# Row maxima of two query heads from one pair of 64-row products, in a two-layer hybrid mixer on one core

## The chip, the cores and the metric

The kernel runs on one core of one Trainium2 chip. The metric is device time in microseconds (us), the median of several runs; less is better.

## What is computed

The reference is two layers over 2048 latent tokens behind a prefix of 256 context tokens, model width 1024. Each layer normalises and modulates the tokens, projects them once, feeds four token mixers (Fourier, attention, short convolution, pooling), gates each with a SiLU path and sends all through one output projection. What the change touches is the attention: 4 query heads of width 64 on 2 key/value heads, latent queries reading all 2304 keys in one softmax.

```python
sc = jnp.einsum('bqkgd,bskd->bkgqs', qi, k_all, preferred_element_type=jnp.float32)
p = jax.nn.softmax(sc, axis=-1).astype(v_all.dtype)
return jnp.einsum('bkgqs,bskd->bqkgd', p, v_all)
```

## The kernel before, in words

Every fp32 operand is split into a high and a low fp16 part, and a product is made of several fp16 products. The tokens are five blocks: block 0 is the 256 context tokens, blocks 1 to 4 hold 512 latent tokens each. In layer 0 attention runs for blocks 1, 2, 3, 4, 0, in layer 1 for blocks 1 to 4.

Attention of one head on one block has two parts. `Head.front` (line 910) loads the head's queries (tile `qb`: high, high, low parts, 192 columns a token), transposes the first 128 columns (line 917) into `qhh` with 128 rows (the high part twice), and finds each query's maximum over all keys: for each of the four groups of 128 queries, five products (line 926) of `qhh` with the keys, one of 256 context keys (`kc`) and four of 512 (`kst`). A key tile has 128 rows, the high part over the low part, so one 128-row product sums query-high by key-high and query-high by key-low. Each product goes into a bank of the pool `mx`, which has two buffers of one bank, and VectorE reduces it to one column of `mp` (line 927). Then the five columns are reduced (line 930), scaled into column 192 of `qb` (line 931), and four more transposes (line 934) give `qlm`, 65 rows: the low query part and the maximum, which one further copy (line 936) brings to SBUF. `Head.main` (line 945) then goes over 18 key tiles of 128 keys: two score products (lines 967 and 968, the second reads `qlm`), two exponentials on ScalarE (`ph` line 972, `p32` line 973), a subtraction on GpSimd or VectorE (`pl`, line 974), and products with the values (lines 962 and 960).

`attention` (line 1014) weaves the heads: while head i runs its `main`, the `front` of head i+1 is advanced at key tiles 0, 2, 4, 7, 10 and 13, a group of 128 queries (five products) at a time, so the last piece of the front comes five key tiles ahead of its use. `spread` (line 1172) weaves in a fill: projections of the other mixers (line 307), later the output projection (line 1120). `opening` (line 1193) starts the first front while the last keys and values of the layer are still being brought in by `keys_values`. In the end a scheduler that simulates the engines sets the order of the instructions on each engine from these streams; each engine then runs its own list in order.

The other names in the change: `gain` and `cd` are constant tiles held for the whole kernel, `z` the buffers of the gate projections, `ot` a buffer of the output projection, `PSHIFT` the headroom that is added to the maximum, `kd` the keys in HBM.

Of the kernel before, what the change touches and what calls it, by code (L numbers as in the profile page):

```python
# [10 lines left out]
F32 = mybir.dt.float32  # L11
# [8 lines left out]
DEPTH = 2  # L20
# [15 lines left out]
PSHIFT = 13.0 * math.log(2.0)  # L36
# [6 lines left out]
def hybrid_kernel(ctx: ExitStack, tc: tile.TileContext, T, out):  # L43
# [12 lines left out]
    banks = {tag: pool("ps_" + tag, 2, space=PSUM) for tag in ("st", "mx", "pv", "fl")}  # L56

    def ring(*tags):
        i = [0]

        def bank(dt=F32):
            i[0] += 1
            tag = tags[i[0] % len(tags)]
            return banks[tag].tile([128, 2048 // mybir.dt.size(dt)], dt, tag=tag, name=tag)

        return bank
# [13 lines left out]
    kd = tc.dram_tile([18, 128, 256], F16, name="kd")  # L80
# [24 lines left out]
    gain = const.tile([128, DEPTH, 4, 64], F32, name="gain")  # L105
    edge = const.tile([128, 2, 16], F32, name="edge")
    invw = const.tile([128, 2], F32, name="invw")
    cd = const.tile([128, 2, 128], F32, name="cd")
# [235 lines left out]
    def token_groups(L, tp, ws):  # L344
# [27 lines left out]

        gm = sm.tile([128, 1], F32, tag="gm", name="gm")
        DVE.tensor_reduce(out=gm, in_=gain[:, L, 0, :], axis=AX.X, op=ALU.max, apply_absolute_value=True)
# [6 lines left out]
        gq = tp.tile([128, 4, 64], F32, tag="gq", name="gq")  # L381
        DVE.tensor_scalar(out=gq[:, 0:2], in0=gain[:, L, 0:2], scalar1=gs, scalar2=None, op0=ALU.mult)
        DVE.tensor_scalar(out=gq[:, 2:4], in0=gain[:, L, 2:4], scalar1=gk, scalar2=None, op0=ALU.mult)
# [45 lines left out]
        def keys(w, b, table):  # L429
            g0, n = BLK[b]  # L430
            nt = n // 128
            q3 = normed(tok_major(w[0], b).rearrange("p t (h f) -> p t h f", h=2), w[1], table)
            o = tp.tile([128, 4, 2, 2, 64], F16, tag="ko", name="ko")[:, 0:nt]
            oh = o[:, :, :, 0, :].rearrange("p t h f -> p (t h) f")
            ol = o[:, :, :, 1, :].rearrange("p t h f -> p (t h) f")
            ACT.copy(out=oh, in_=q3)
            POOL.tensor_tensor(out=ol, in0=q3, in1=oh, op=ALU.subtract)
            SP.dma_start(out=kd[g0 // 128:(g0 + n) // 128].rearrange("t p c -> p t c"), in_=o.rearrange("p t h s f -> p t (h s f)"))
# [221 lines left out]
    def fourier(L, tp):  # L660
        def ub(shape, dt, name):
            return tp.tile(shape, dt, tag="u", name=name)

        wf = ub([128, 2, 256], F32, "wf")
# [192 lines left out]
    def keys_values(L, tp, kvs):  # L857
# [19 lines left out]
        for b in range(5):  # L877
# [3 lines left out]
            kr = tp.tile([128, 4, 256], F16, tag="zt", name="kr")[:, 0:nt]  # L881
            SP.dma_start(out=kr, in_=kd[t0:t0 + nt].rearrange("t p c -> p t c"))
            for kv in range(2):
                pt = mx_bank(F16)
                for t in range(nt):
                    mark[0] = PE.transpose(out=pt[:, t * 128:(t + 1) * 128], in_=kr[:, t, kv * 128:(kv + 1) * 128], identity=id16).ins
                if b == 0:
                    ACT.copy(out=kc_[:, 0, kv, :], in_=pt[:, 0:n])
                    DVE.tensor_copy(out=kc_[0:64, 1, kv, :], in_=pt[0:64, 0:n])
                else:  # L890
                    ACT.copy(out=kst[kv][:, g0 - NCTX:g0 - NCTX + n], in_=pt[:, 0:n])
                    DVE.tensor_copy(out=k2[kv][0:64, g0 - NCTX:g0 - NCTX + n], in_=pt[0:64, 0:n])
# [8 lines left out]

    class Head:


        def __init__(self, L, kvs, b, h, tp):
            self.L, self.kvs, self.b, self.h, self.tp = L, kvs, b, h, tp

        def front(self):
            b, h, tp, kvs = self.b, self.h, self.tp, self.kvs
            g0, n = BLK[b]  # L910
            nt = n // 128
            kv = h // 2
            qb = tp.tile([128, 4, QW], F16, tag="qb", name="qb")[:, 0:nt]
            load_mark[0] = SP.dma_start(out=qb[:, :, 0:192], in_=qd[g0 // 128:(g0 + n) // 128, :, h].rearrange("t p c -> p t c")).ins
            pt = mx_bank(F16)
            for t in range(nt):
                PE.transpose(out=pt[:, t * 128:(t + 1) * 128], in_=qb[:, t, 0:128], identity=id16)
            qhh = tp.tile([128, 512], F16, tag="qhh", name="qhh")[:, 0:n]
            ACT.copy(out=qhh, in_=pt[:, 0:n])
            yield  # L920
            keys = [kvs["kc"][:, 0, kv, :]] + ([] if b == 0 else [kvs["kst"][kv][:, i * 512:(i + 1) * 512] for i in range(4)])
            mp = sm.tile([128, 4, 5], F32, tag="mp", name="mp")
            for t in range(nt):
# [5 lines left out]
            mr = sm.tile([128, 4], F32, tag="mr", name="mr")[:, 0:nt]  # L929
            DVE.tensor_reduce(out=mr, in_=mp[:, 0:nt, 0:len(keys)], axis=AX.X, op=ALU.max)  # L930
            DVE.tensor_scalar(out=qb[:, :, 192], in0=mr, scalar1=-1.0 / MROW, scalar2=PSHIFT * LOGIT / MROW, op0=ALU.mult, op1=ALU.add)
            pt = mx_bank(F16)
            for t in range(nt):
                PE.transpose(out=pt[0:65, t * 128:(t + 1) * 128], in_=qb[:, t, 128:193], identity=id16)
            qlm = tp.tile([128, 512], F16, tag="qlm", name="qlm")[:, 0:n]
            DVE.tensor_copy(out=qlm[0:65, :], in_=pt[0:65, 0:n])
            self.q = qhh, qlm
# [7 lines left out]
        def main(self):  # L945
# [4 lines left out]
            qhh, qlm = self.q  # L950
# [35 lines left out]
        def back(self, o32):  # L986
# [3 lines left out]
            if h % 2 == 0:  # L990
                o32[0] = tp.tile([128, 4, 128], F32, tag="o32", name="o32")[:, 0:nt]
            o = o32[0]
# [6 lines left out]
        def close(self, o32):  # L999
# [3 lines left out]
            o = o32[0]  # L1003
            if h % 2:
                j = h // 2
                zt = tp.tile([128, 512], F32, tag="zt", name="zt")[:, 0:n]
# [7 lines left out]
    def attention(heads):  # L1014

        o32 = [None]
        for _ in heads[0].front():
            yield
        for i, hd in enumerate(heads):
            ahead = heads[i + 1].front() if i + 1 < len(heads) else iter(())  # L1020
            for j, _ in enumerate(hd.main()):
                if j == 1 and i:
                    heads[i - 1].back(o32)
                if j == (1 if heads[i].b == 0 else 3) and i:
                    heads[i - 1].close(o32)
                if hd.b == 0 or j in (0, 2, 4, 7, 10, 13):
                    next(ahead, 0)
                yield
            yield from ahead
        heads[-1].back(o32)  # L1030
        heads[-1].close(o32)
# [60 lines left out]
    def project(L, blocks, tp):  # L1092
# [13 lines left out]
        for i, tok in enumerate(toks):  # L1106
# [9 lines left out]
            for half in range(2):  # L1116
# [8 lines left out]
                ot = tp.tile([128, 512], F32, tag="ot", name="ot")  # L1125
# [230 lines left out]
```

## Time and profile before

| | |
|---|---|
| median of 3 runs | 2284.16 us (2273.7 to 2284.55) |
| the profiled execution's own time | 2278.62 us |
| its span, first to last instruction | 2276.8 us |
| TensorE busy | 2169.0 us, 95% of the span |
| VectorE busy | 1401.3 us, 62% |
| ScalarE busy | 1228.4 us, 54% |
| GpSimd busy | 929.4 us, 41% |
| mean granted TensorE clock | 0.979 of full |

In the rows further down PE is TensorE's matmul part, PEld its weight loads, DVE VectorE, ACT ScalarE, POOL GpSimd, SP the queue that issues most DMAs. A matmul's shown duration contains its way through the pipeline, so the distance between two starts is what a matmul takes from the engine, and the duration is when its result is there.

### The profile page before, as it was taken

The numbers are of one execution on the slowest core, as the hardware profiler recorded it, in microseconds if no ns is written. First come the engines' busy times: TensorE is split into PE (matmuls) and PEld (weight loads), VectorE is DVE, ScalarE is ACT, GpSimd is POOL, SyncE is SP. The second block draws the span as 40 slices with busy tenths as digits, with TensorE's granted clock in tenths as the row PEclk, the third lists the DMA queues.
The fourth block names the chain that finished last, engine by engine and source line by source line (L and its number), as shares of the span: only waits on it lengthen the run. The fifth ranks groups of instructions, "written<-read, shape, count | busy, mean of one in ns | idle before, by whom it ended". The sixth has DMA issues, their size and how long they took to land.

```text
span 2276.8 us, 41305 instructions
## 1 busy us (share of the span) xinstructions
PE 2169.0 (95%) x16327; PEld 1296.6 (57%) x16327; DVE 1401.3 (62%) x2639; ACT 1228.4 (54%) x2297; POOL 929.4 (41%) x996
## 2 busy tenths in 40 slices
PE   7998999989998999999999989999999999899999
PEld 3997556545555555545557984554454555455554
DVE  3655686366768767666465546413567767687743
ACT  4653453346777666544545625323467666566640
POOL 2786443214444455422226861011344556333320
PEclk9999999999999999999999999999999999899999
DMA  8423455510322111223473424323124210222133
GB/s 316 149 87 120 148 183 177 176 57 24 108 83 81 45 36 33 91 86 110 147 241 124 136 73 139 112 104 103 35 70 143 68 37 31 65 72 73 61 116 120
DMA packets 164081, 237.97 MB, mean 105 GB/s; under 512 B 28618, under 2 KB 113966, under 8 KB 163886
## 3 DMA queue, kind: packets, MB, share of 16 engines
q1 hardware_dynamic: 141294, 205.95, 27.2%
q10 hardware_dynamic: 22592, 29.37, 4.2%
q8 instruction: 128, 2.10, 0.4%
q14 instruction: 67, 0.55, 0.1%
HBM read 165.94 MB, written 69.34 MB: 103 GB/s over the span
## 4 chain that ended last, share of the span: by engine, by line
PE 75%; DVE 8%; POOL 6%; ACT 5%; DMA 3%; issue 3%; SPq 0%; POOLq 0%; ACTq 0%; DVEq 0%
PE fl L307 19%; PE fl L1120 15%; PE st L307 6%; PE pv L962 4%; PE st L967 4%; PE mx L926 4%; PE st L968 4%; PE pv L329 3%; PE st L329 3%; PE pv L960 2%; DVE mp L927 2%; PE st L319 2%; PE pv L319 2%; PE mx L848 1%; PE fl L169 1%
## 5 line engine op out<-in xcount | busy, mean ns | idle before, releaser
L307 PE MATMUL fl<-h,w 128*128 128x512 f16 (+1 forms) x2592 | 585.4, 372 | 12.5 <-ACT w L147 8.9
L974 POOL TENSOR_TENSOR pl<-p,ph 128x512 f16<-128x512 f32 (+1 forms) x292 | 360.4, 1234 | 566.1 <-ACT p L973 488.5
L307 PEld LDWEIGHTS <-w 128*128 128x128 f16 x3456 | 332.3, 99 | 376.6 <-issue 23.7
L972 ACT ACTIVATE ph<-st 128x512 f16<-128x512 f32 (+1 forms) x584 | 350.9, 601 | 233.4 <-PE st L968 225.0
L927 DVE TENSOR_REDUCE mp<-mx 128x1 f32<-128x512 f32 (+1 forms) x648 | 390.2, 627 | 123.6 <-PE mx L926 115.7
L1120 PE MATMUL fl<-wo,ml 128*128 128x512 f16 x1632 | 376.5, 379 | 1.3 <-DVE ml L148 0.8
L973 ACT ACTIVATE p<-st 128x512 f32<-128x512 f32 (+1 forms) x584 | 351.5, 602 | 30.2 <-DVE pl L974 22.7
L974 DVE TENSOR_TENSOR pl<-p,ph 128x512 f16<-128x512 f32 (+1 forms) x292 | 232.5, 796 | 123.5 <-ACT p L973 103.5
L1120 PEld LDWEIGHTS <-ml 128*128 128x128 f16 x1632 | 157.4, 98 | 181.7 <-DVE ml L148 1.4
L962 PE MATMUL pv<-V,ph 128*128 128x130 f16 x2320 | 231.1, 222 | 6.3 <-ACT ph L972 5.8
L962 PEld LDWEIGHTS <-ph 128*128 128x128 f16 x2320 | 170.9, 98 | 115.5 <-ACT ph L972 27.7
L926 PE MATMUL mx<-kst,qhh 128*128 128x512 f16 x512 | 192.3, 387 | 21.6 <-DVE mp L927 20.7
L967 PE MATMUL st<-qhh,kst 128*128 128x512 f16 x512 | 196.4, 384 | 6.4 <-ACT p L973 5.6
L968 PE MATMUL st<-qlm,k 65*128 65x512 f16 x512 | 197.4, 386 | 0.0
L307 PE MATMUL st<-h,w 128*128 128x512 f16 (+1 forms) x864 | 191.0, 372 | 0.0
L960 PE MATMUL pv<-V,pl 128*128 128x66 f16 x2320 | 173.0, 194 | 11.7 <-POOL pl L974 5.8
L960 PEld LDWEIGHTS <-pl 128*128 128x128 f16 x2320 | 134.8, 98 | 63.7 <-POOL pl L974 12.1
L329 PEld LDWEIGHTS <-h 128*128 128x128 f16 x1632 | 159.4, 98 | 19.5 <-POOL h L269 0.7
L319 PEld LDWEIGHTS <-h 128*128 128x128 f16 x1728 | 98.9, 98 | 1.3 <-issue 0.6
L926 PEld LDWEIGHTS <-qhh 128*128 128x128 f16 x648 | 62.9, 99 | 63.2 <-issue 24.0
L329 PE MATMUL pv<-w,h 128*128 128x256 f16 x816 | 94.3, 274 | 0.4 <-POOL h L269 0.4
L269 POOL TENSOR_TENSOR h<-h,h 128x512 f16<-128x512 f32 x72 | 85.3, 1189 | 18.3 <-ACT h L268 17.4
(303 smaller groups left out, 2906.1 us busy)
## 6 DMA issues: line engine op xcount, KB each, us to landing
wm<-in_w_mod_dram SPq DMA_DIRECT2D x48, 512.0 KB, 4.7
wst<-in_w_in_dram SPq DMA_DIRECT2D x44, 512.0 KB, 4.8
mix<-mixd SPq DMA_DIRECT2D x34, 512.0 KB, 4.2
zd<-z SPq DMA_DIRECT2D x64, 256.0 KB, 2.2
wst<-in_w_out_dram SPq DMA_DIRECT2D x32, 512.0 KB, 4.8
xt<-in_x_dram SPq DMA_DIRECT2D x20, 512.0 KB, 4.8
xd<-xt SPq DMA_DIRECT2D x18, 512.0 KB, 2.9
xt<-xd ACTq DMA_DIRECT2D x18, 512.0 KB, 3.6
```

What stands on the lines that cost most here:

```text
L307: PE.matmul(out=ps, lhsT=w[:, wp, k, :], rhs=h_ap(b, hp, k, 0, n), start=(k == 0 and i == 0), stop=(k == KC - 1 and i == 2))
L329: PE.matmul(out=ps[:, t], lhsT=h_ap(b, hp, k, (2 * i + t) * 128, 128), rhs=w[:, :, wp, k, :], start=(k == 0 and j == 0), stop=(k == KC - 1 ...
L926: mark[0] = PE.matmul(out=ps, lhsT=qhh[:, t * 128:(t + 1) * 128], rhs=kk, start=True, stop=True).ins
L927: DVE.tensor_reduce(out=mp[:, t, i:i + 1], in_=ps, axis=AX.X, op=ALU.max)
L960: PE.matmul(out=pv[t // 2][:, t % 2, 0:66], lhsT=p, rhs=v[:, 0:66], start=False, stop=(kt == nk - 1), skip_group_check=True)
L962: PE.matmul(out=pv[t // 2][:, t % 2, :], lhsT=p, rhs=v, start=(kt == 0 and t % 2 == 0), stop=False, skip_group_check=True)
L967: mark[0] = PE.matmul(out=ps, lhsT=self.k_tile(0, kt), rhs=qhh, start=True, stop=False).ins
L968: PE.matmul(out=ps, lhsT=self.k_tile(1, kt)[0:65, :], rhs=qlm[0:65, :], start=False, stop=True)
L972: ACT.activation(out=ph, in_=ps, func=ACTF.Exp, scale=1.0 / LOGIT)
L973: ACT.activation(out=p32, in_=ps, func=ACTF.Exp, scale=1.0 / LOGIT)
L974: (POOL if kt % 2 == 0 else DVE).tensor_tensor(out=pl, in0=p32, in1=ph, op=ALU.subtract)
L1120: PE.matmul(out=ps, lhsT=ml[:, mp, k, :], rhs=wo[k][:, wp, half * 512:(half + 1) * 512], start=(k == 0 and j == 0), stop=(k == KC - 1 and ...
```

## The change

A class `Pair` takes the place of `Head.front`. It makes the front of two query heads, i and i+2, which belong to the two key/value heads. The key tile of head 1 is turned over (low part over high part, which needs the high part once more in HBM: `kd` has 320 columns for 256), so that key head 0 has its high part in rows 0 to 63 and key head 1 in rows 64 to 127. The maximum is now taken over the products of the high parts alone, 64 rows each: head i in the upper half of the array, head i+2 in the lower, into the two banks of one tile, and one reduction takes the maxima of both. The low part is left out of the maximum, and `PSHIFT` goes from 13 to 10 powers of two. `mx` becomes one buffer of two banks during attention (`mx_mode`). The front advances one pair of products at a time, spread over both heads' key tiles. Three front steps, no longer one, go with each step of `opening`. `qb` has one buffer (of two heads), `z` and `pw` one, `gain` and `cd` are loaded anew in each layer, and `ot` is gone (the product with the gate is written back to PSUM). Line numbers from here on with 948, 949, 957 and the like are those of the changed kernel.

```diff
-PSHIFT = 13.0 * math.log(2.0)
+PSHIFT = 10.0 * math.log(2.0)
...
+    def mx_mode(name, wide):
+        mx_scope.close()
+        p = mx_scope.enter_context(tc.tile_pool(name="ps_mx" + name, bufs=1 if wide else 2, space=PSUM, reuse_waits="tile"))
+        banks["mx"], banks["size"] = p, 4096 if wide else 2048
...
+            DVE.tensor_copy(out=o[:, :, 256:320], in_=pairs[:, :, 1, 0, :])
...
+            def turned(c, m):
+                pt = pv_bank(F16)
                 for t in range(nt):
-                    mark[0] = PE.transpose(out=pt[:, t * 128:(t + 1) * 128], in_=kr[:, t, kv * 128:(kv + 1) * 128], identity=id16).ins
+                    mark[0] = PE.transpose(out=pt[0:m, t * 128:(t + 1) * 128], in_=kr[:, t, c:c + m], identity=id16).ins
+                return pt
+            pt = turned(0, 128)
+            ACT.copy(out=both[0], in_=pt[:, 0:n])
+            DVE.tensor_copy(out=high[0][0:64], in_=pt[0:64, 0:n])
+            pt = turned(192, 128)
+            ACT.copy(out=both[1], in_=pt[:, 0:n])
+            pt = turned(128, 64)
+            DVE.tensor_copy(out=high[1][0:64], in_=pt[0:64, 0:n])
...
+    class Pair:
+        def __init__(self, b, i, tp, kvs):
+            self.b, self.heads, self.tp, self.kvs = b, (i, i + 2), tp, kvs
+            self.nt, self.nk = BLK[b][1] // 128, 1 if b == 0 else 5
+            self.steps = 1 + self.nt * self.nk
...
+            mp = sm.tile([128, 2, 4, 5], F32, tag="mp", name="mp")
+            for t in range(nt):
+                for j in range(nk):
+                    ps = mx_bank().rearrange("p (h c) -> p h c", h=2)[:, :, 0:512 if j else NCTX]
+                    for i in range(2):
+                        kk = kvs["kst"][i][:, (j - 1) * 512:j * 512] if j else kvs["kc"][:, 0, i, :]
+                        r = slice(64 * i, 64 * i + 64)
+                        mark[0] = PE.matmul(out=ps[:, i], lhsT=qhh[r, i, t * 128:(t + 1) * 128], rhs=kk[r], start=True, stop=True).ins
+                    DVE.tensor_reduce(out=mp[:, :, t, j], in_=ps, axis=AX.X, op=ALU.max)
+                    yield
...
-            for t in range(nt):
-                for i, kk in enumerate(keys):
-                    ps = mx_bank()[:, 0:kk.shape[-1]]
-                    mark[0] = PE.matmul(out=ps, lhsT=qhh[:, t * 128:(t + 1) * 128], rhs=kk, start=True, stop=True).ins
-                    DVE.tensor_reduce(out=mp[:, t, i:i + 1], in_=ps, axis=AX.X, op=ALU.max)
-                yield
...
-                if hd.b == 0 or j in (0, 2, 4, 7, 10, 13):
-                    next(ahead, 0)
-                yield
-            yield from ahead
+                    at += 1
+                    while done < want * at // (total - 1):
+                        next(ahead, 0)
+                        done += 1
+                    yield
...
-        for i, _ in enumerate(load):
-            if i < 5:
-                steps(att, 1)
+        for _ in load:
+            steps(att, 3)
             yield 1
...
-        ap = TagPool(right, tc, f"a{L}", {"zt": 2, "p32": 2, "qb": 2, "qhh": 2, "qlm": 2, "ph": 3, "pl": 3, "acc": 1, "o32": 1}, "right")
+        ap = TagPool(right, tc, f"a{L}", {"zt": 2, "p32": 2, "qb": 1, "qhh": 2, "qlm": 2, "ph": 3, "pl": 3, "acc": 1, "o32": 2}, "right")
+        mx_mode(f"a{L}", True)
```

The order moves at two places that matter below. The first is TensorE's list while attention opens in layer 0. Names: `kst` and `kc` are keys, `qhh` queries, `w` a weight of the fill, `h` its tokens; what stands in brackets is the engine that is waited for. Before:

```order
L926 LDWEIGHTS qhh
L926 MATMUL mx<-kst_5482,qhh 128x512 [waits DVE_49]
L926 LDWEIGHTS qhh
L926 MATMUL mx<-kst_5482,qhh 128x512 [waits DVE_49]
L307 LDWEIGHTS w
L307 MATMUL fl<-h_322,w 128x256
```

The change, at the same stage:

```order
L948 LDWEIGHTS qhh
L948 MATMUL mx<-kst_5494,qhh 128x512 [waits DVE_49]
L948 LDWEIGHTS qhh
L948 MATMUL mx<-kst_5495,qhh 128x512
L948 LDWEIGHTS qhh
L948 MATMUL mx<-kst_5494,qhh 128x512 [waits DVE_49]
L948 LDWEIGHTS qhh
L948 MATMUL mx<-kst_5495,qhh 128x512
L315 LDWEIGHTS w
L315 MATMUL fl<-h_318,w 128x256
```

Two products that fill the two buffers became two products that fill one; the next pair waits for VectorE to have read both. In the changed list the 324 pairs stand in 304 runs: 293 single pairs and 11 runs of two to four pairs, with 21 places where a pair stands straight behind another; 20 of these places are in the two openings.

The second place is TensorE's list where a front ends and the next one begins. `qb` is loaded by DMA, `id` is the identity of a transpose. Before, four transposes to `qlm` (line 934), at once the four of the next head's `qb`, then fill:

```order
L934 LDWEIGHTS qb
L934 MATMUL mx<-id_98,qb 65x128
L917 LDWEIGHTS qb [waits DMAHW7_49]
L917 MATMUL mx<-id_98,qb 128x128
L917 LDWEIGHTS qb
L917 MATMUL mx<-id_98,qb 128x128
L917 LDWEIGHTS qb
L917 MATMUL mx<-id_98,qb 128x128
L917 LDWEIGHTS qb
L917 MATMUL mx<-id_98,qb 128x128
L307 LDWEIGHTS w
L307 MATMUL fl<-h_1461,w 128x512 [waits Activation_49]
```

The change, at one of its 20 such places (line 957 is what line 934 was, 998 what 968 was, 992 what 962 was, 937 what 917 was):

```order
L957 LDWEIGHTS qb
L957 MATMUL mx<-id_98,qb 65x128
L998 LDWEIGHTS kc
L998 MATMUL st<-qlm,kc 128x512 [waits DVE_49]
L998 LDWEIGHTS kc
L998 MATMUL st<-qlm,kc 128x512
L992 LDWEIGHTS ph [waits Activation_49]
L992 MATMUL pv<-V_5485,ph 128x130 [waits PE_49]
```

Behind these rows come three more products of line 992 and then the transposes of line 937, whose `qb` can be loaded only when the transposes of line 957 have read the one buffer. The score products that read `qlm` now follow its transposes directly, and the next load and its use stand within a few products of each other.

## Rows read from the trace of the kernel before

**Rows 1.** The page: busy time of TensorE's matmuls, and the chain that ended last.

```profile
PE 2169.0 (95%) x16327; PEld 1296.6 (57%) x16327; DVE 1401.3 (62%) x2639; ACT 1228.4 (54%) x2297; POOL 929.4 (41%) x996
...
PE 75%; DVE 8%; POOL 6%; ACT 5%; DMA 3%; issue 3%; SPq 0%; POOLq 0%; ACTq 0%; DVEq 0%
```

**Rows 2.** Groups by line and shape: count, busy us, mean ns, idle before and releaser.

```profile
L926 PE MATMUL mx<-kst,qhh 128*128 128x512 f16 x512 | 192.3, 387 | 21.6 <-DVE mp L927 20.7
...
L926 PE MATMUL mx<-kc,qhh 128*128 128x256 f16 x136 | 37.8, 279 | 4.7 <-ACT qhh L919 2.7 <-DVE mp L927 1.9
```

**Rows 3.** Timeline of TensorE, 800 to 818 us: start, length, instruction.

```profile
800.49 0.27 PE L926 MATMUL mx<-kc,qhh 128*128 128x256 f16 x1
800.60 0.22 PE L960 MATMUL pv<-V,pl 128*128 128x66 f16 x2
...
802.34 0.38 PE L926 MATMUL mx<-kst,qhh 128*128 128x512 f16 x1
802.56 0.39 PE L962 MATMUL pv<-V,ph 128*128 128x130 f16 x4
```

**Rows 4.** TensorE's waits, whole span: us in total, times, longest.

```profile
PE mx L926 <- DVE mp L927: 22.6, 53, 2.5
...
PE st L968 <- DVE qlm L936: 1.1, 4, 0.3
```

**Rows 5.** The same in the opening of layer 0 (450 to 560 us).

```profile
PE mx L926 <- DVE mp L927: 1.8, 6, 0.6
```

**Rows 6.** The same in the opening of layer 1 (1560 to 1650 us).

```profile
PE mx L926 <- DVE mp L927: 3.0, 10, 0.6
```

**Rows 7.** Timeline of TensorE near the start, where the array's used shape changes (rows*columns).

```profile
15.16 1.02 PE L169 MATMUL fl<-wm,sc 128*2 128x512 f32 x2
...
15.59 0.59 PE L169 MATMUL fl<-wm,sc 128*2 128x512 f32 x1
...
16.12 0.22 PE L186 MATMUL mx<-id,row 2*128 2x2 f32 x1
...
31.61 0.49 PE L261 MATMUL fl<-id,xn 128*128 128x128 f32 x3
...
31.83 0.27 PE L261 MATMUL fl<-id,xn 128*128 128x128 f32 x1
...
32.03 0.59 PE L169 MATMUL fl<-wm,sc 128*2 128x512 f32 x1
```

**Rows 8.** Timeline of TensorE and VectorE in layer 0's opening and later: products and maxima.

```profile
483.01 0.59 PE L926 MATMUL mx<-kst,qhh 128*128 128x512 f16 x2
...
483.42 2.48 DVE L927 TENSOR_REDUCE mp<-mx 128x1 f32<-128x512 f32 x4 [0.16 <-PE mx L926]
484.17 0.38 PE L926 MATMUL mx<-kst,qhh 128*128 128x512 f16 x1 [0.57 <-DVE mp L927]
...
807.33 0.42 DVE L927 TENSOR_REDUCE mp<-mx 128x1 f32<-128x256 f32 x1 [2.31 <-PE mx L926]
...
471.88 1.28 DVE L148 SCALAR_TENSOR_TENSOR w<-wst,ws,w 128x1024 f16<-128x1024 f32 x1
```

**Rows 9.** Timeline at the end of the first front: maximum to first product that reads it.

```profile
491.38 0.17 DVE L930 TENSOR_REDUCE mr<-mp 128x4 f32<-128x20 f32 x1
491.59 0.18 DVE L931 TENSOR_SCALAR qb<-mr 128x4 f16<-128x4 f32 x1
...
493.01 0.39 PE L934 MATMUL mx<-id,qb 128*65 128x128 f16 x4
...
493.44 0.42 DVE L936 COPY qlm<-mx 65x512 f16<-65x512 f16 x1 [1.67 <-PE mx L934]
...
493.91 0.59 PE L968 MATMUL st<-qlm,kc 65*128 65x512 f16 x2 [0.29 <-DVE qlm L936]
```

**Rows 10.** DMA issues by line: count, KB each, median us from issue to landing.

```profile
qb<-qd SPq DMA_DIRECT2D x32, 192.0 KB, 2.6
```

**Rows 11.** Timeline of TensorE: eight transposes of keys in `keys_values`.

```profile
460.05 0.61 PE L886 MATMUL mx<-id,kr 128*128 128x128 f16 x8
```

More of the change, by code (lines that the diff above doesn't have):

```diff
@@ L63, in bank @@
             tag = tags[i[0] % len(tags)]
-            return banks[tag].tile([128, 2048 // mybir.dt.size(dt)], dt, tag=tag, name=tag)
+            size = banks["size"] if tag == "mx" else 2048
+            return banks[tag].tile([128, size // mybir.dt.size(dt)], dt, tag=tag, name=tag)
         return bank
@@ L432, in keys @@
             q3 = normed(tok_major(w[0], b).rearrange("p t (h f) -> p t h f", h=2), w[1], table)
[L433 to L438, printed above, removed]
+            o = tp.tile([128, 4, 320], F16, tag="ko", name="ko")[:, 0:nt]
+            pairs = o[:, :, 0:256].rearrange("p t (h s f) -> p t h s f", h=2, s=2)
+            q4 = q3.rearrange("p (t h) f -> p t h f", h=2)
+            ACT.copy(out=pairs[:, :, :, 0, :], in_=q4)
+            POOL.tensor_tensor(out=pairs[:, :, :, 1, :], in0=q4, in1=pairs[:, :, :, 0, :], op=ALU.subtract)
+            DVE.tensor_copy(out=o[:, :, 256:320], in_=pairs[:, :, 1, 0, :])
+            SP.dma_start(out=kd[g0 // 128:(g0 + n) // 128].rearrange("t p c -> p t c"), in_=o)
         def queries(w, b, i, table):
@@ L662, in ub @@
             return tp.tile(shape, dt, tag="u", name=name)
+        cd = tp.tile([128, 2, 128], F32, tag="cd", name="cd")
+        SP.dma_start(out=cd, in_=T["k_cd"])
         wf = ub([128, 2, 256], F32, "wf")
@@ L949, in main @@
             kv = h // 2
-            qhh, qlm = self.q
+            qhh, qlm = (q[:, self.i] for q in self.pair.q)
             nk = 2 if b == 0 else 18
@@ L1012, in close, with attention @@
                 SP.dma_start(out=mixd[MO_A + j, :, g0:g0 + n], in_=zt)
[L1014 to L1025, printed above, removed]
-                if hd.b == 0 or j in (0, 2, 4, 7, 10, 13):
-                    next(ahead, 0)
-                yield
-            yield from ahead
-        heads[-1].back(o32)
-        heads[-1].close(o32)
+    def attention(L, kvs, pairs):
+        o32 = {}
+        yield from pairs[0].front()
+        last = None
+        for p, pair in enumerate(pairs):
+            after = pairs[p + 1] if p + 1 < len(pairs) else None
+            ahead, want = (after.front(), after.steps + 1) if after else (iter(()), 0)
+            total, at, done = 2 * (2 if pair.b == 0 else 18), 0, 0
+            for i in range(2):
+                hd = Head(L, kvs, pair, i)
+                for j, _ in enumerate(hd.main()):
+                    if j == 1 and last:
+                        last.back(o32)
+                    if j == (1 if hd.b == 0 else 3) and last:
+                        last.close(o32)
+                    at += 1
+                    while done < want * at // (total - 1):
+                        next(ahead, 0)
+                        done += 1
+                    yield
+                last = hd
+            for _ in ahead:
+                pass
+        last.back(o32)
+        last.close(o32)
     wo, gate, fm = [], {}, {}
@@ L1124, in project @@
                 h = slice(half * 512, (half + 1) * 512)
[L1125 to L1127 removed]
+                DVE.tensor_tensor(out=ps, in0=ps, in1=gate[0][:, h], op=ALU.mult)
+                DVE.tensor_tensor(out=xt[:, h], in0=xt[:, h], in1=ps, op=ALU.add)
             SP.dma_start(out=out[tok - NCTX:tok - NCTX + 128] if L == DEPTH - 1 else xd[tok:tok + 128], in_=xt)
@@ L1151, in hybrid_kernel @@
                     ws += [load_w(0, *TOKEN_W[0])]
-        SP.dma_start(out=gain, in_=T["gains"].partition_broadcast(128))
         ws += [load_w(0, *TOKEN_W[1])]
```

101 lines of the change are left out of this document (47 added, 54 removed).

## The prediction

> **What bounds the kernel now.** I read the page first. TensorE is busy for 95% of the span and the chain that ended last runs on it for 75% [rows 1]; no other engine holds a tenth of that chain. So what counts is the time that an edit takes from or gives to TensorE's own list, which it works off in order: a wait of one product there holds up everything behind it, the fill included. The timeline of TensorE then gives what a product costs inside a dense stretch, from start to start: 0.22 us for 512 columns (802.34 to 802.56) and 0.11 us for 256 (800.49 to 800.60) [rows 3]. The groups by shape give the counts of the maximum's products, 512 wide ones and 136 of 256 columns [rows 2], and the waits say that VectorE already holds them up, 22.6 us in 53 waits [rows 4], of which 1.8 and 3.0 us lie in the two openings [rows 5, 6]. The sum below is made against the profiled execution's own 2278.62 us, which lies 5.5 us under the median of 2284.16. A measurement of this kernel can tell about 0.5% from no change, 11.4 us.
>
> **What the change takes away on TensorE.** 648 products become 324 pairs, 256 wide and 68 of 256 columns. If the two halves of a pair run side by side, a pair costs what one product did, so 256 x 0.22 + 68 x 0.11 = 64 us go. No row of before shows two products side by side. The bounds are this and nothing gained; I take the gain, because the two products share neither rows of the array nor partitions of an operand nor a bank. The Trainium skill, "TensorE: Matmul & The Clock Gate", Part 3 on packing, says that products in different row groups run concurrently and start some 4 ns apart; by that the gain would be about 1 us less than mine, and no run here shows it yet.
>
> **What it adds there: changes of the array's shape.** A pair uses the array as two halves of 64 rows, and the products around it use it whole. The trace of before has a few changes of shape, near the start. In front of one, a product of line 169 (two columns of the array in use) starts at 15.16 us and the next at 15.59, 0.43 apart, but the following one of another shape (line 186) starts only 0.53 after that, at 16.12: 0.10 us more. The whole array behaves alike: transposes of line 261 are 0.11 apart ((0.49 - 0.27) / 2), and from the last of them, at 31.83, to a product of line 169 it is 0.20: 0.09 more [rows 7]. The 324 pairs stand in 304 runs, so there are 608 changes, at 0.095 us 58 us. The bounds are 0 (a change between whole and half rows may cost nothing, and no row has just that one) and 61 us at 0.10; I take 58, since these are the only rows with a change of shape and they agree with each other. The Trainium skill, "TensorEngine Tiling (Array Packing)", Key Properties, states that a change of the tiling mode, not of the tile alone, drains TensorE; the trace agrees with its 0.09 to 0.10 us for other modes, and by that rule 64-row products between 128-row ones pay at both ends. Products and changes of shape together so come to -6 us: nearly all of the gain is spent.
>
> **Keys.** The turned keys need 36 more transposes, at (0.61 - 0.22) / 7 = 0.056 us [rows 11] 2 us, and ten groups of them use 64 columns, 20 changes of shape or 2 us: +4.
>
> **One buffer in place of two.** Before, two products lay in two banks and VectorE read one while the other was written. From a product's start to its maximum's start it took 0.41 us (483.01 to 483.42), a wide maximum took 0.68 us (0.60 from start to start), and 0.07 us after its end (484.10) the next product started, at 484.17 [rows 8]. A maximum over both banks has 1024 elements a row. No such one is there; a 256 column maximum takes 0.42 us, so 256 elements cost 0.26 and the wide one is 0.68 + 0.52 = 1.20 us. The other end is 1.28, what another VectorE operation takes for 1024 elements [rows 8]; I take 1.20, from the same operation. Now a pair can start only 0.41 + 1.20 + 0.07 = 1.68 us after the one before it. Where a pair stands straight behind another, TensorE has only 0.22 us of work in that time and stands for 1.46 us; with 256 columns it is 0.30 + 0.68 + 0.07 = 1.05 us, of which it stands 0.94. There are 21 such places, 17 and 4: 25 + 4 = 29 us, and 4.8 us of waits of the openings before [rows 5, 6] go: +24.
>
> Elsewhere one pair at a time stands among other products. Counting the columns between two runs at 0.42 ns each (0.22 us / 512), 18 of the 303 stretches are too short if VectorE is free when the pair is done, by 5 us in all, and 85 by 38 us if it has just begun another operation of 0.6 us. The 17.9 us of such waits that lay outside the openings before (22.6 - 4.8) go. So -13 to +20; I take +3, about the middle.
>
> **Where a front ends.** There are 20 such places for 36. The last piece of a front comes one key tile ahead of its use, where it was five. Three waits follow. (1) From the transposes to the first score product that reads `qlm` it took 0.90 us (493.01 to 493.91) with four transposes and a copy of 0.42 us [rows 9]; with eight, and a copy of twice the columns (0.42 to 0.84, taken 0.78), it is about 1.5, and TensorE has 0.45 us of transposes in it. In 9 of 20 places nothing stands between: 9 us, less the 1.1 us there were [rows 4]. (2) From the last pair to the transposes: 0.41 + 1.20 + 0.39 us for the two small operations (491.38 to 491.77) [rows 9] and a tenth for the hand-overs make 2.1 us; in 7 places too little stands between, short by 7 us in all, some of which was there before: +5. (3) `qb` has one buffer, so its load begins when the last transposes have read it, and lands 2.6 us after its issue [rows 10]. With two loads issued one behind the other and the eight transposes ahead that is 3.3 us. Six places have 0.66 us of products in that time, and after wait (1) TensorE is still short by 1.5 us in each; four others by 3 us together: +12. The load waits on SP's queue meanwhile, and behind it stand loads of the fill (`zp`, `zc`), whose use is some products away; I cost that at nothing. Together +25; bounds 8 (half of the places covered, the loads early) and 35.
>
> **At nothing.** VectorE's maxima shrink from 648 to 324; it is off TensorE's list but for the waits above. `z` with one buffer: a gate group of 24 products takes 5 us, its store less. `ot` gone: the second operation reads PSUM a little longer, with two banks for 5 us of products each. `gain`, `cd` and 64 more columns of `kd`: DMAs of a few microseconds at most, the first two once a layer, in front of work that waits for other loads. If that cover is gone, 1 to 2 us a layer.
>
> **Sum.** -64 + 58 + 4 + 24 + 3 + 25 = +50 us. Some of the new waits fall together with old ones in the openings (weights, `qhh`), where TensorE stood anyway: -5. So 2278.6 + 45 = 2324, and with a part of the distance to the median **2326 us**, 1.8% slower. The forecast's own range is 2295 to 2358, from the ends above.
>
> **Rivals.**
> (A) *Changing between whole and half rows is free.* The other changes of shape in the trace involve two columns or two rows of the array and fp32; this one does not. Then 58 us fall away: 2326 - 58 = 2268, 0.7% faster. It decides by the cost of one change: at 608 changes the kernel is level with 2284 where one costs 0.026 us, against the 0.095 of the rows. Beside it stands the page "TensorEngine Tiling (Array Packing)", Theoretical Speedup, which gives up to 2x for a contraction of 64 rows or fewer; that is this case's 64 us, with nothing taken off.
> (B) *The waits are covered.* If the list leaves enough work around each pair, what remains is -64 + 58 + 4 + 3 = +1, and the time is 2280 to 2286: no change. For it: the order comes from a simulation that knows of the one buffer, and half of the places where a front ends have 1 to 6 us of products in between. Against it: the 21 pairs that stand straight behind another have nothing to cover them.
> (C) *The halves do not run side by side*, so the change does not do what it says: +64, 2390 us. For it, no row of before shows an overlap; against it, nothing shared is known.
>
> **Chances.** Forecast 0.58, A 0.20, B 0.14, C 0.08. The range reaches from A to the forecast's upper end, 2264 to 2358, and leaves out C and half-way mixtures above it. Faster by over 0.5% is A, 0.20; within it is B, 0.14; slower is the forecast and C, 0.66.
>
> **What would show it.** Right: the second product of a pair starts within some 0.05 us of the first; the product behind a pair starts 0.3 us or more after it, not 0.22; a maximum takes 1.2 us; TensorE's waits for line 949 rise from 22.6 to some 45 us, with about 1.4 us each in the openings; waits for `qlm` and `qb` at several ends of fronts, near 1 us each. Wrong: products around a pair follow at 0.22 us (A), a pair's second product starts 0.22 us after the first (C), or TensorE's idle time stays near the 108 us that it was (2276.8 - 2169.0) (B).

## The result and the profile after

The changed kernel takes **2351.55 us** (median of 4 runs, 2349.03 to 2353.28) against 2282.07 for the kernel before beside it: a ratio of 1.0317, 95% interval 1.03 to 1.0334. The way was forecast and the time lies in the range, 25.6 us above the predicted 2326. The profiled execution has a span of 2347.2 us, 70.4 more than before, and a mean granted clock of 0.970 (0.979 before). Of all executions below one is slow, one of the four of two_whole (3231.11 us at a granted clock of 0.65): the 2313.75 us given for that kernel is the median of all four, and that of the other three is 2312.23.

The page of the changed kernel: busy time, to be held against [rows 1], and the products and maxima by line, against [rows 2] (count, busy, mean ns, idle before and its releaser):

```profile
PE 2197.4 (94%) x16363; PEld 1271.8 (54%) x16363; DVE 1361.4 (58%) x2271; ACT 1227.9 (52%) x2279; POOL 921.5 (39%) x996
...
L949 DVE TENSOR_REDUCE mp<-mx 128x2 f32<-128x1024 f32 (+1 forms) x324 | 359.6, 1110 | 186.9 <-PE mx L948 185.5
...
L948 PE MATMUL mx<-kst,qhh 64*128 64x512 f16 x512 | 102.5, 396 | 28.8 <-DVE mp L949 27.4
```

The 70.4 us fall into two parts. TensorE's idle time rises from 107.8 us (2276.8 - 2169.0) to 149.8 (2347.2 - 2197.4), by 42.0; its busy time rises by 28.4, although the same work is in it but for the halves, the keys and the changes of shape. The busy time of the wide products of the maximum falls from 192.3 us [rows 2] to 102.5 (line 948), in half as many places; it contains their way through the pipeline, so it is not what TensorE gains.

TensorE's waits over the whole span (us in total, times, longest), to be held against [rows 4]:

```profile
PE mx L948 <- DVE mp L949: 32.0, 33, 2.0
PE pv L992 <- ACT ph L1002: 20.9, 28, 2.2
...
PE pv L901 <- ACT kst L908: 8.1, 7, 1.7
PE mx L937 <- DMA qb<-qd: 7.3, 11, 1.5
PE st L998 <- DVE qlm L959: 6.7, 8, 1.2
...
PE mx L957 <- DVE qb L953: 5.2, 6, 2.2
...
PE pv L990 <- POOL pl L1004: 3.2, 6, 0.8
```

The same list of the kernel before, where the lines are 926 (waits for the maximum, 22.6 us [rows 4]), 962, 960 and 934:

```profile
PE pv L962 <- ACT ph L972: 5.8, 12, 0.8
PE pv L960 <- POOL pl L974: 5.8, 8, 1.6
...
PE pv L960 <- DVE pl L974: 5.3, 8, 1.8
...
PE mx L934 <- DVE qb L931: 2.4, 2, 1.2
```

The waits for the maximum rise by 9.4 us only. In the two openings they rise from 4.8 us [rows 5, 6] to 25.0. These are their rows, the first for 450 to 570 us, the second for 1590 to 1690 us:

```profile
PE mx L948 <- DVE mp L949: 14.1, 11, 2.0
```

```profile
PE mx L948 <- DVE mp L949: 10.9, 9, 1.3
```

Elsewhere they fall from 17.9 to 7.0 us. What has grown besides are the waits for `ph`, for the keys' copies (line 901, there were none before), and at the ends of fronts (`qb`, `qlm`).

**A pair in a dense stretch.** Timeline of TensorE in the changed kernel, start, length, instruction:

```profile
800.88 0.38 PE L998 MATMUL st<-qlm,k 65*128 65x512 f16 x1
801.20 0.39 PE L948 MATMUL mx<-kst,qhh 64*128 64x512 f16 x2
801.52 0.40 PE L992 MATMUL pv<-V,ph 128*128 128x130 f16 x4
```

Two products together last 0.39 us, as long as one alone [rows 3], so the halves do run side by side. But the pair starts 0.32 us after the product ahead of it, and the next product 0.32 after the pair, where products without a change follow at 0.22 [rows 3]. A change of shape costs 0.10 us at each end. It is so all over the trace: at full clock, where nothing waits, the median is 0.10 us in front of a pair (272 places) and 0.11 behind it (281). The pair takes 0.42 us out of the list (0.64 less the 0.22 of the product ahead), and two whole products took 0.44.

**Pairs behind one another.** Timeline of layer 0's opening, TensorE and VectorE:

```profile
482.59 0.39 PE L948 MATMUL mx<-kst,qhh 64*128 64x512 f16 x2
484.30 0.39 PE L948 MATMUL mx<-kst,qhh 64*128 64x512 f16 x2 [1.32 <-DVE mp L949]
486.01 0.61 PE L948 MATMUL mx<-kst,qhh 64*128 64x512 f16 x2 [1.32 <-DVE mp L949]
...
501.82 5.40 PE L315 MATMUL fl<-h,w 128*128 128x256 f16 x18
```

```profile
483.02 1.23 DVE L949 TENSOR_REDUCE mp<-mx 128x2 f32<-128x1024 f32 x1 [0.43 <-PE mx L948]
484.73 1.23 DVE L949 TENSOR_REDUCE mp<-mx 128x2 f32<-128x1024 f32 x1 [0.48 <-PE mx L948]
```

A maximum over 1024 elements takes 1.23 us (predicted 1.20), and a pair can start 1.71 us after the one before it (predicted 1.68). The third pair is 0.61 us long. The 18 fill products at 501.82 us are six of 256 columns and twelve of 512 (the row names the first shape alone); they take 5.40 us, where 6 x 0.11 + 12 x 0.22 = 3.3 us would be the distance of their starts in a dense stretch [rows 3]. Both are the granted clock. The same stretch by window; columns are start and end, length, busy us and count of PE, PEld, DVE, ACT and POOL, then the granted clock, the DMA share and GB/s. First the kernel before, then the changed one:

```profile
443.00:530.00 87.00, 79.40 (x539) 44.23 (x537) 49.82 (x102) 41.72 (x77) 19.72 (x29) 0.94 0.20 60
```

```profile
443.00:530.00 87.00, 63.88 (x336) 32.34 (x333) 40.10 (x66) 20.40 (x34) 5.92 (x17) 0.80 0.17 51
```

```profile
485.00:501.00 16.00, 10.09 (x48) 5.44 (x48) 8.22 (x9) 1.47 (x4) 1.58 (x5) 0.62 0.03 9
501.80:505.80 4.00, 4.00 (x15) 1.96 (x14) 0.69 (x1) 0.00 (x0) 0.00 (x0) 0.50 0.00 0
505.90:507.20 1.30, 1.30 (x8) 0.45 (x7) 0.00 (x0) 0.00 (x0) 0.00 (x0) 1.00 0.00 0
507.00:516.00 9.00, 5.91 (x30) 2.17 (x29) 4.90 (x4) 2.29 (x3) 1.03 (x2) 1.00 0.00 0
```

In the same 87 us TensorE has 336 matmuls where it had 539. From 485 to 501 us, where pairs wait for pairs, the mean granted clock is 0.62 of full, nearer its lower level (0.50, 1.2 GHz) than its upper one (2.4 GHz). It is still at the lower level in the fill behind, where TensorE stands no more, until about 505.8 us, and 1.00 from there on. Over the span the clock holds back (1 - 0.970) x 2347.2 = 70 us, before (1 - 0.979) x 2276.8 = 48 us, idle time included. Added up from the trace's record of the clock, TensorE is busy at the lower level for 114.7 us, before for 74.7. A product takes twice as long there (last section), so half of the 40 us more, about 20 of the 28.4 us by which busy time rose, are the clock's.

**Keys.** Timeline of `keys_values` in layer 0:

```profile
447.91 0.61 PE L901 MATMUL pv<-id,kr 128*128 128x128 f16 x8
449.45 0.38 PE L901 MATMUL pv<-id,kr 128*64 128x128 f16 x4 [0.94 <-ACT kst L908]
```

The pool `pv` has two banks. Eight transposes fill them, and the four new ones of 64 columns stand until ScalarE has copied one of them out.

### The profile page after: what moved, and what is told of

It reads as the page before. It is cut to its first block, busy times and chain, and to the rows that moved or that the text cites. A ratio compares the mean times of both kernels' runs of the same rounds, so it can differ in the third digit from the quotient of the medians.

```text
span 2347.2 us, 40945 instructions
## 1 busy us (share of the span) xinstructions
PE 2197.4 (94%) x16363; PEld 1271.8 (54%) x16363; DVE 1361.4 (58%) x2271; ACT 1227.9 (52%) x2279; POOL 921.5 (39%) x996
## 5 line engine op out<-in xcount | busy, mean ns | idle before, releaser
L315 PE MATMUL fl<-h,w 128*128 128x512 f16 (+1 forms) x2592 | 605.6, 380 | 12.4 <-ACT w L155 8.9
L949 DVE TENSOR_REDUCE mp<-mx 128x2 f32<-128x1024 f32 (+1 forms) x324 | 359.6, 1110 | 186.9 <-PE mx L948 185.5
L992 PE MATMUL pv<-V,ph 128*128 128x130 f16 x2320 | 231.9, 223 | 21.5 <-ACT ph L1002 20.9
L948 PE MATMUL mx<-kst,qhh 64*128 64x512 f16 x512 | 102.5, 396 | 28.8 <-DVE mp L949 27.4
L1163 DVE TENSOR_TENSOR fl<-fl,gate 128x512 f32<-128x512 f32 x68 | 47.5, 698 | 109.8 <-PE fl L1158 109.7
L327 PEld LDWEIGHTS <-h 128*128 128x128 f16 x1728 | 99.1, 98 | 0.8
L948 PEld LDWEIGHTS <-qhh 64*128 64x128 f16 x648 | 33.3, 93 | 113.9 <-issue 98.2
```

The costliest lines, as they stand in the source:

```text
L315: PE.matmul(out=ps, lhsT=w[:, wp, k, :], rhs=h_ap(b, hp, k, 0, n), start=(k == 0 and i == 0), stop=(k == KC - 1 and i == 2))
L948: mark[0] = PE.matmul(out=ps[:, i], lhsT=qhh[r, i, t * 128:(t + 1) * 128], rhs=kk[r], start=True, stop=True).ins
L949: DVE.tensor_reduce(out=mp[:, :, t, j], in_=ps, axis=AX.X, op=ALU.max)
L992: PE.matmul(out=pv[t // 2][:, t % 2, :], lhsT=p, rhs=v, start=(kt == 0 and t % 2 == 0), stop=False, skip_group_check=True)
```

## The experiments

Ten kernels, all edits of the changed one, timed against the kernel before. The first theory says that the time went to the one buffer (openings and elsewhere), to the ends of fronts, and to changes of shape that eat up the gain of the halves. The rivals are named in each expectation.

**whole_rows: the whole array again, all else as in the change.** 128-row products into the same two-bank tile; the maximum is then taken over what it was taken over before.

```diff
-                        r = slice(64 * i, 64 * i + 64)
-                        mark[0] = PE.matmul(out=ps[:, i], lhsT=qhh[r, i, t * 128:(t + 1) * 128], rhs=kk[r], start=True, stop=True).ins
+                        mark[0] = PE.matmul(out=ps[:, i], lhsT=qhh[:, i, t * 128:(t + 1) * 128], rhs=kk, start=True, stop=True).ins
```

> The pairs' products use all 128 rows again (as the kernel before did), everything else as in the changed kernel: two-bank tile, weave, order of 303 runs. Theory: the halves save 62 us of products and cost 0.095 us at each of some 600 changes of shape, 57 us, so nothing much is lost: 2357 us (2345 to 2370). Rival 1: the changes of shape are free and the whole loss lies in waits: 2351.6 + 62 = 2413. Rival 2: the changes cost twice what the spacings show: under 2310.

Measured: 2350.56 us, 1.031 [1.0285, 1.0335], against 2351.55. Halves are worth nothing here. Timeline of TensorE in this kernel:

```profile
809.73 0.25 PE L989 MATMUL pv<-V,pl 128*128 128x66 f16 x3
809.82 0.59 PE L947 MATMUL mx<-kst,qhh 128*128 128x512 f16 x2
810.25 0.19 PE L989 MATMUL pv<-V,pl 128*128 128x66 f16 x1
```

Two whole products take 0.43 us (809.82 to 810.25) with no change of shape around them; the pair of halves took 0.42 with both changes. Busy time differs by 1.9 us in 2197.4.

**two_tiles: two buffers of one bank again, 64-row products kept.** Each product goes into its own tile and has its own maximum.

```diff
-                    ps = mx_bank().rearrange("p (h c) -> p h c", h=2)[:, :, 0:512 if j else NCTX]
+                    pss = [mx_bank()[:, 0:512 if j else NCTX] for _ in range(2)]
...
-                    DVE.tensor_reduce(out=mp[:, :, t, j], in_=ps, axis=AX.X, op=ALU.max)
+                    for i in range(2):
+                        DVE.tensor_reduce(out=mp[:, i, t, j:j + 1], in_=pss[i], axis=AX.X, op=ALU.max)
...
-        mx_mode(f"a{L}", True)
+        mx_mode(f"a{L}", False)
```

> The two halves' products go into two tiles of one bank with a maximum each, as before; the 64-row products stay. In the order most products of a pair no longer stand together (512 runs for 304). Theory: the one buffer's waits go (some -35 us with the clock), but 416 more changes of shape at 0.095 us cost +40 us and some 200 products no longer lie beside their partner, +44 us: about 2400 us (2375 to 2420). Rival: the one buffer is the whole cause and changes of shape are cheap: near 2290.

**two_whole: the same with 128-row products** (the edits of whole_rows and two_tiles together).

> As two_tiles (two tiles of one bank, a maximum each), but with products of all 128 rows, so without any change of shape at the maxima. The order stands as there, 514 runs. Theory: 1024 changes of shape at 0.095 us go, -97 us; the some 115 pairs that still stood together lose their overlap, +24 us: 2390 -> 2317 us (2305 to 2330). Rival: changes of shape cost nothing and two_tiles lost its time elsewhere: 2390 to 2415.

Measured: two_tiles 2389.96 us, 1.0489 [1.0469, 1.0508]; two_whole 2313.75, 1.0165 [1.0134, 1.0196]. They differ in the shape of the products alone, by 76 us. In the order of two_tiles the 648 products stand in 512 runs, so only 136 have a neighbour to run beside, and there are 1024 changes of shape. Of the 136, by the starts in the trace, 88 do run beside it (59 wide, 29 narrow); the others wait for a buffer or for the product ahead. A lone 64-row product, timeline of two_tiles:

```profile
799.94 0.38 PE L999 MATMUL st<-qlm,k 65*128 65x512 f16 x1
800.16 1.46 PE L315 MATMUL fl<-h,w 128*128 128x512 f16 x6
801.55 0.39 PE L948 MATMUL mx<-kst,qhh 64*128 64x512 f16 x1
801.87 1.47 PE L315 MATMUL fl<-h,w 128*128 128x512 f16 x6
```

From its start to the next product it takes 0.32 us, and the six ahead take 1.39 (800.16 to 801.55) where 6 x 0.22 is 1.32. With 88 products gained, 59 x 0.22 + 29 x 0.11 = 16 us, one change costs (76 + 16) / 1024 = 0.090 us. That is the price of [rows 7], in another way. Page of two_tiles, then of two_whole, which shows that the 76 us are TensorE's busy time (78.7) and not waits:

```profile
PE 2262.9 (95%) x16363; PEld 1275.5 (53%) x16363; DVE 1395.0 (59%) x2595; ACT 1234.9 (52%) x2279; POOL 925.9 (39%) x996
```

```profile
PE 2184.2 (94%) x16363; PEld 1303.3 (56%) x16363; DVE 1395.6 (60%) x2595; ACT 1230.3 (53%) x2279; POOL 924.4 (40%) x996
```

And from whole_rows to two_whole, one buffer of two banks against two of one, it is 2350.56 - 2313.75 = 37 us: the price of the one buffer, with what the clock adds to it (0.970 against 0.977). The traces tell the two apart: of the 37.4 us between the spans (2350.9 and 2313.5) 22.3 are idle time, and some 14 are the clock, half of the 119.3 - 91.7 us by which TensorE is busy at the lower level for longer. What stays of two_whole over the kernel before, 1.65%, lies in the rest of the change: the new weave, the keys and the ends of fronts, or the smaller buffers and the second loads of `gain` and `cd`.

**opening1: one front step per step of `opening`, as before,** for the first five, the rest by `spread`.

```diff
-        for _ in load:
-            steps(att, 3)
+        for i, _ in enumerate(load):
+            if i < 5:
+                steps(att, 1)
             yield 1
...
-            n, m = 72 * len(early) + 3, 8 * 4 * nb + 3 + m - 15 - 18
+            n, m = 72 * len(early) + 16, 8 * 4 * nb + 3 + m - 15 - 18
```

> The opening again advances the first front by one step in five of its six load steps (three in each of the six in the changed kernel); the other pairs of the first front come among the fill. Theory: the two openings, cleared of the fill that moved into them, cost 30 and 20 us, of which some 29 us is idle time behind the one buffer and some 14 us the halved clock; most of it goes, 2351.6 -> 2305 us (2295 to 2320), waits of line 948 from 32 to under 15 us, and the granted clock near 1.00 where it was 0.79 (455 to 535 us). Rival: each pair waits for its maximum wherever it stands, so the waits only move: 2345 to 2355.

Measured: 2330.13 us, 1.0222 [1.0196, 1.0249]: 21 us back, between what theory and rival expected. Its window over layer 0's opening:

```profile
443.00:530.00 87.00, 70.13 (x412) 36.20 (x413) 43.00 (x70) 25.83 (x47) 10.55 (x22) 0.94 0.21 65
```

The clock is back at the 0.94 of before, and 412 products are done in the time, not yet 539. Of the 27 us of span (the profiled execution is the fastest of the four) 14.2 are busy time (2197.4 to 2183.2) and 12.9 idle; busy time at the lower level falls from 114.7 to 87.0 us, and half of that is nearly all of the 14.2. So the openings' waits cost about as much again through the clock as they do by themselves. The waits for the maximum are still 22.4 us, and those for `qlm` rise to 11.0: the coarse opening was not all.

**opening_busy: the first front's waits filled with work that nobody reads.** Behind each maximum of the first front the program has three 64-row products into a bank of `pv`, 120 in all. In TensorE's list they do not always stand there: in 13 of the 40 pairs of the two first fronts, two or three of them stand between the two products of the pair.

```diff
+            self.first = False
...
+                    if self.first:
+                        idle = pv_bank()
+                        for _ in range(3):
+                            PE.matmul(out=idle, lhsT=qhh[r, 1, t * 128:(t + 1) * 128], rhs=kvs["kst"][1][r, 0:512], start=True, stop=True)
...
+        pairs[0].first = True
```

> Adds work: behind each pair of the first front in a layer, three more 64-row products into a spare pv bank that nothing reads, 120 in all, 26 us of TensorE's time, of which some 18 us fit into the waits for the one buffer. Theory (the waits pull the granted clock down and so cost a second time): the clock stays at or near full in the opening of layer 0, where 34 us ran at half clock, which gives back up to 12 us and pays for the 8 us that don't fit: 2346 us (2340 to 2352), that opening's stretch shorter than 86 us. Rival (the clock is of no account): 2352 + 8 = 2360 us or more, that stretch 90 us.

Measured: 2363.23 us, 1.0396 [1.0362, 1.0429], 12 us slower than the change: the rival's time, though not its reason. The windows that tell what happened, 485 to 516 us, first the change, then this kernel:

```profile
485.00:516.00 31.00, 21.51 (x96) 10.06 (x96) 14.25 (x14) 3.76 (x7) 2.62 (x7) 0.72 0.01 5
```

```profile
485.00:516.00 31.00, 25.73 (x135) 11.87 (x133) 14.48 (x14) 1.47 (x4) 1.58 (x5) 0.89 0.01 5
```

The granted clock does rise, from 0.72 to 0.89. Busy time over the span is 2216.0 us; without the 120 x 0.22 = 26.4 us added it is 2189.6, 7.8 less than in the change, and idle time falls by 9.9 (149.8 to 139.9). So more work in the waits brings the clock up, but 17.7 us back do not pay for 26.4 put in. By the record of the clock, busy time at the lower level falls by 10.9 us, worth some 5.5, so that the products put in cost rather 24 us than 26.4. The clock's share is real, and it was not bought back this way.

**keys_mx: the third group of key transposes into `mx`,** which is idle then.

```diff
-                pt = pv_bank(F16)
+                pt = pv_bank(F16) if m == 128 else mx_bank(F16)
```

> The third group of key transposes (64 columns) takes its tile from mx and not from pv, whose two banks the first two groups hold. Theory: its waits for the copies of those two (9.0 us in the changed kernel, kst and kc) go: 2351.6 -> 2343 us (2338 to 2347). Rival: the next transposes then wait for the same copies: no change, 2348 to 2355.

Measured: 2334.42 us, 1.0267 [1.0235, 1.0298]: 17 us back for ten groups, 36 transposes. Timeline of TensorE in this kernel, where nothing stands between the groups any more:

```profile
452.33 0.61 PE L901 MATMUL pv<-id,kr 128*128 128x128 f16 x8
452.87 0.41 PE L901 MATMUL mx<-id,kr 128*64 128x128 f16 x4
453.21 1.04 PE L315 MATMUL fl<-h,w 128*128 128x512 f16 x4
```

The waits taken away were 9.0 us (8.1 for `kst`, 0.9 for `kc`). Idle time falls by 6.8 us and busy time by 10.5 (2197.4 to 2186.9), with a mean clock of 0.975 for 0.970 (busy at the lower level for 99.1 us, not 114.7). Again a wait in the openings is worth about twice its length.

**front_early: the last piece of a front five key tiles ahead of its use,** as in the kernel before; in the change it is one.

```diff
-                    while done < want * at // (total - 1):
+                    while done < want * at // (total - (5 if pair.b else 1)):
```

> The front ends four key tiles earlier. Theory: the waits at its end (qlm 6.7 us, the maximum in qb 5.2, the load of qb 7.3, together 19 us in the changed kernel) fall to some 6: 2338 us (2332 to 2346). Rival: the pairs stand closer together (22 steps in 31 key tiles, not 35), so waits for the one buffer take their place: 2348 to 2358.

Measured: 2350.44 us, 1.0317 [1.0292, 1.0342], no change. Two waits of this kernel:

```profile
PE mx L948 <- DVE mp L949: 39.0, 37, 2.5
...
PE mx L937 <- DMA qb<-qd: 3.3, 8, 0.9
```

The waits for `qb` fall from 7.3 to 3.3 us, and those for `qlm` from 6.7 to 5.0, but the same steps in fewer key tiles stand closer to one another, and the waits for the maximum rise from 32.0 to 39.0. With one buffer an earlier end only moves the waits: the rival was right for this edit alone.

**combined, combined_whole, combined_two_whole.** The three edits of order (opening1, keys_mx, front_early) together: with the change's own 64-row pairs; with whole_rows; and with two_whole.

> opening1, keys_mx and front_early together: the best that the changed kernel's own plan gives. Theory: 2330 less 8 (keys) less 4 (end of fronts, now that the opening no longer stands in the way): 2318 us (2308 to 2326), still slower than before, since the products themselves give nothing. Rival (the halves do give time, and waits hide it): under 2285.

> The combined kernel with products of all 128 rows in the two-bank tile. Theory: as between the changed kernel and whole_rows, the halves save as much as their changes of shape take, 2306 us (2298 to 2314). Rival: with the waits mended the halves' 62 us shows: 2340 or more.

> The combined kernel with two tiles of one bank and products of all 128 rows: neither the halves nor the two-bank tile of the change are left, its pairs, weave and key layout stay. Theory: the one buffer costs what whole_rows and two_whole showed between them (2350.6 - 2313.8 = 37 us with the clock, here less, since the openings are mended): 2306 - 28 = 2278 us (2268 to 2290), level with the kernel before. Rival: what is left over the kernel before (29 us) lies in the weave, the single qb and the keys: 2295 to 2306.

| | order of the change | with the three edits of order |
|---|---|---|
| 64-row pairs, one two-bank tile | 2351.55 (the change) | 2305.63 (combined), 1.0137 [1.0108, 1.0166] |
| 128-row products, one two-bank tile | 2350.56 (whole_rows) | 2307.23 (combined_whole), 1.0128 [1.0097, 1.0159] |
| 128-row products, two one-bank tiles | 2313.75 (two_whole) | **2267.89** (combined_two_whole), 0.9951 [0.9928, 0.9975] |

The kernel before took 2276.89 to 2282.07 us beside them, so a difference between two cells can be off by some 5 us. Within that the three parts add up, in whichever row or column they are read. Whole rows in place of halves: -1 and +2 us, which is nothing. One buffer against two: 37 and 39. The order: 46, 43 and 46. The last kernel beats the kernel before by 0.5%; it has neither the halves nor the two-bank tile. It keeps the front of two heads at once, in single steps, and the smaller buffers and second loads, which so cost little unless something else gives as much back. Its busy time and its waits for the maximum:

```profile
PE 2164.0 (95%) x16363; PEld 1296.7 (57%) x16363; DVE 1381.5 (61%) x2595; ACT 1227.8 (54%) x2279; POOL 926.2 (41%) x996
```

```profile
PE mx L947 <- DVE mp L949: 18.7, 38, 2.0
```

Idle time is 102.3 us (span 2266.3), below the 107.8 of before, and the granted clock 0.986. The waits for `ph`, 20.9 us in the change, are 7.1.

## Why the prediction was right, and where its sum was off

**Products and changes of shape, -64 + 58: right, both terms.** The pair lasts as long as one product, a change costs 0.10 us at each end, and whole_rows and combined_whole show that nothing is left of the gain. Rival A (a change between whole and half rows is free) falls by the row at 801.20 us, rival C (the halves one after the other) by the same row. The Trainium skill, "TensorEngine Tiling (Array Packing)", Theoretical Speedup, gives up to 2x for 64 rows; for a pair of 512 columns between whole products the runs show no gain. The Trainium skill, same page, Key Properties, says that a change of the tiling mode drains TensorE, and the 0.10 us at both ends of a pair agree with that.

**One buffer in the openings, +24: right by its rows.** The cycle is 1.71 us for 1.68, and waits of the openings rise by 20.2 us (25.0 - 4.8). **Elsewhere, +3: too dark,** it was -11 (17.9 to 7.0); the work between single pairs covers the longer maximum. That is why the sign that was named, some 45 us of waits for line 949, did not come: they are 32.0.

**Ends of fronts, +25: it was 15.7,** within the bounds of 8 to 35. The waits for `qlm` rise by 5.6 us (predicted 8), for `qb` from the small operations by 2.8 (5), for the load of `qb` by 7.3 (12).

**Keys, +4: this step failed.** It counted the time of the transposes and not the bank that they wait for. Three groups now share two banks of `pv`, which makes 9.0 us of waits, and taking them away gave 17. Rule: with one more writer in a rotation of buffers, the count of buffers belongs in the sum.

**What the sum had no term for.** All in all it had +47 us of idle time (24 + 3 + 25 - 5), and 42.0 came, though of another make: 9.4 for the maximum, 15.7 at ends of fronts, 9.0 for keys, 15.1 for `ph` (5.8 to 20.9), and 7 less in the rest, of which 5.8 in the waits for `pl`. That the totals lie so near is luck: the maximum and the ends of fronts brought 25.1 us for the 47 of the sum, and the waits for keys and for `ph`, which had no term, brought 24.1. It had -2 us of busy time, and +28.4 came. This is the miss. About 20 us of it are the granted clock, which the prediction took as it was: every wait was costed at its own length, while the opening's stretch, with waits of 1.3 us between pairs, ran at 0.62. opening1 and keys_mx, which shorten waits in the openings, each gave back about as much busy time as idle time. The prediction's row for it was there: the 0.979 of before is a mean, and a sum that puts 20 us of waits in one place must ask what the clock does in that place and behind it. The other 8.4 us are no matter of the clock, and the sum had -2; whole_rows has 8.0 by the same reckoning, so the gain of 6 us that was left to the halves did not come, and some 4 us stay open.

**Rival B (waits covered)** was right for the maximum outside the openings and wrong for the whole: idle time is 149.8 us, not near 108.

**What stays open.** Why TensorE waits 15 us more for `ph`: ScalarE's two exponentials a key tile are 0.60 us each, and where neither fill nor a maximum lies in a key tile TensorE is done sooner. In the trace of the change 19 of these waits follow straight on a score product of line 998, before none did so; but this is argued, and no run changed it alone. It falls to 11.3 us in opening1 and 11.8 in two_tiles, so it hangs on the order of the list. The single `qb` was not tried with two buffers, nor were the smaller buffers by themselves.

## What to carry to other kernels

Packing two half-height products side by side saves one product's time and pays a change of shape on either side; with 0.22 us saved and 2 x 0.10 paid, a lone pair between whole-array products is worth nothing. By the same sum halves would pay in runs of several pairs, which no run here tried. One wide buffer in place of two narrow ones turns each hand-over into a full round trip (here 1.71 us), which is covered only where other work stands between: count the places where two users follow one another. And cost a cluster of waits on TensorE at more than its length: the granted clock falls in it, and the dense work behind it runs slow for some microseconds more (four, in the stretch shown).

## What the runs showed of the hardware beyond expectation

At the lower level of the clock a dense stretch takes just twice its time, weight loads included. The fill products behind the pair at 501.49 us, the six narrow ones and then five of the wide ones, at a granted clock of 0.50 (window 501.80 to 505.80):

```profile
501.82 1.46 PE L315 MATMUL fl<-h,w 128*128 128x256 f16 x6
503.07 2.34 PE L315 MATMUL fl<-h,w 128*128 128x512 f16 x5
```

The six narrow products start at 501.82 and the first wide one at 503.07, so a narrow one takes 1.25 / 6 = 0.21 us, where one takes 0.11 in a dense stretch at full clock [rows 3]. Two of the weight loads of the wide ones in that stretch:

```profile
503.50 0.15 PEld L315 LDWEIGHTS <-w 128*128 128x128 f16 x1 [0.28 <-issue]
503.93 0.15 PEld L315 LDWEIGHTS <-w 128*128 128x128 f16 x1 [0.28 <-issue]
```

They come 0.43 us apart, as the wide products do, and that is twice the 0.22 of full clock. So the loads still lie under the products here, and the lower level costs the factor of the clock and no more.

The halves of the array also run beside each other when they belong to different steps. Timeline of opening_busy:

```profile
485.29 0.39 PE L954 MATMUL pv<-kst,qhh 64*128 64x512 f16 x1
485.30 0.39 PE L949 MATMUL mx<-kst,qhh 64*128 64x512 f16 x1
```

A filler product in the lower half and the next pair's first product in the upper half start 0.01 us apart, into different banks.
